# First 512 features of the modulation vector in two halves, with six weight blocks begun between them

## The chip, the cores and the metric

The kernel runs on one core of one Trainium2 chip. A core has a matrix engine (TensorE; PE in the profile, with its weight loads as PEld), a vector engine (VectorE, DVE), a scalar engine (ScalarE, ACT), a general engine (GpSimd, POOL) and a queue engine (SyncE, SP) that here only issues DMAs. Each engine runs its own instructions in the order in which they were written for it, and waits where an instruction needs a result of another engine or a transfer. POOL issues DMAs too, on a queue of its own.

The metric is the time of one execution on the device, in microseconds (us). Three runs of the kernel before took 1944.65, 1945.36 and 1946.12 us; the median is 1945.36 us.

## The reference

One transformer layer on 256 rows of 2048 features, all in float32. A vector c of 2048 numbers gives nine vectors of 2048 numbers each (three shifts, three scales, three gates); they set the modulation of the three parts of the layer:

```python
ada = (jax.nn.silu(c) @ w_ada + b_ada)[:, None, :]
sh1, sc1, g1, sh2, sc2, g2, sh3, sc3, g3 = jnp.split(ada, N_ADA, axis=-1)
h = _swiglu(_modulate(x, sh1, sc1), ffn1_w_in, ffn1_w_out)
x = _layernorm(ALPHA * x + 0.5 * (1 + g1) * h, ln1_g, ln1_b)
h = _token_mixer(_modulate(x, sh2, sc2), w_in, ...)
...
def _modulate(x, shift, scale):
    return _layernorm(x) * (1 + scale) + shift
```

`w_ada` is 2048 x 18432, which is 151 MB, and the feed-forward weights `ffn1_w_in` are 2048 x 11264. So the first matmul of the layer cannot begin before some columns of `w_ada` (shift and scale of the first features) were read over all 2048 rows, summed with silu(c), and put on the normalised x.

## The kernel before, in words

**Precision.** Each float32 operand of a large product is split into two rounded parts, hi (a cast on ACT, L142) and lo (a subtraction on DVE, L143). A product is three matmuls, hi·hi, hi·lo and lo·hi (`mm3`, L357 to L359). x after modulation is kept transposed, as 16 k-tiles of 128 features by 256 rows, each with its hi and lo part (`xhi_f`, `xlo_f`; L296 and L299).

**The opening.** The features of the first feed-forward part are taken in four groups j of 512 (four k-tiles each). For the group j = 0, `first_ada0` reads 16 pieces of `w_ada`, one for each 128 rows of it, with 512 shift and 512 scale columns: 512 KB each, issued by SP (L694). The scale columns are summed on DVE (L155, L157, into `gate`), the shift columns on PE, which multiplies each piece by a column of silu(c) (L695, into `row`). When the last piece is in, the sums over the 128 partitions are made on PE as columns (L658 and L660), DVE adds the bias (`scsh`, L662), ACT applies scale and shift to the transposed x (L293) and casts (L296), DVE makes the lo part (L299). Then the products of group 0 begin. Earlier pieces lie in the buffer `hT`, which later takes partial results, in `gate`, and, for the pieces 12 to 14, in the buffers `araw` and `aw`.

**The products of the opening.** For each group j, twelve blocks i of 512 columns of `ffn1_w_in` are multiplied (`first_in`). A block of a group is 4 k-tiles by 4 column tiles by 3 matmuls: 48 matmuls `s<-...` of 256 columns. Its weights (1 MB) come in one DMA of SP into one of three buffers `raw_s`; hi and lo of two k-tiles each have one of six buffers. The result of a block stands in two of five PSUM banks; for j = 0, ACT copies it to `hT` (L765), for j > 0, DVE adds it there (L767).

**Beside the products.** While group j is multiplied, `first_ada(j + 1)` reads the pieces of the next group (512 KB each, issued by POOL, L721), and DVE sums both of their halves (L155, L157, 1024 elements in each partition). POOL has three buffers for them (two `araw`, one `aw`): a piece is issued when the piece three before has been summed. The columns of the next group (L656 here) are put between the matmuls of the eleventh and twelfth block. Later stages (the rest of the feed-forward part, the mixer, the second feed-forward part) follow on PE without the change touching them.

**Order.** The program is written with generators that are stepped by hand (the tuples of small numbers in the loops say how many pieces are stepped after which block), and a scheduler places the instructions of each engine from that; on each engine the order is then fixed.

Of the kernel before, what the change touches and what calls it, by code (L numbers as in the profile page):

```python
# [14 lines left out]
P = 128  # L15
# [17 lines left out]
def layer_kernel(  # L33
# [304 lines left out]
    def load_w(src, nk, w, name, by_parts=False, behind=None):  # L338
# [4 lines left out]
        h = nk // 2 if nk * w <= 2048 else nk // 4  # L343
# [304 lines left out]
    def first_columns(j, acc, mb, ws, shifts=None):  # L648
        cps = aux_tile(f"cp{j}"), mm_tile(f"cq{j}")

        def column(q):
            cp = cps[q % 2][:, q:q + 2]
            qs = slice(q * P, (q + 1) * P)
# [7 lines left out]
            k = 4 * j + q  # L661
# [4 lines left out]
        column(1)  # L666
        next(mb)
        next(mb)
        column(2)
        next(ws, None)  # L670
        next(mb)
        column(3)
        next(mb)
        for _ in mb:
            pass

    def first_ada0(ws):
        src = pair_cols(0, 0)  # L680
        acc = gate[:, :512]
        part = mm_tile("row0")
        shifts = ap.tile([P, 2, 512], F32, tag="acc", name="shifts")[0:1, 0, :]
        spots = [hT[:, 4 * i:4 * i + 4, :].rearrange("p f t -> p (f t)") for i in range(KF // 4)] + [gate[:, 1024:]]
        spots = [r.rearrange("p (v n) -> p v n", v=2) for r in spots]
        for k in range(KD):
            if k in (12, 13):
                raw = ap.tile([P, 2, 512], F32, tag="araw", bufs=2, name=f"ar0_0_{k}")
            elif k == 14:
                next(ws)  # L690
                raw = ep.tile([P, 2, 512], F32, tag="aw", name=f"ar0_0_{k}")
            else:
                raw = spots[k % 15]
            SP.dma_start(raw, src[k * P:(k + 1) * P])  # L694
            PE.matmul(part[0:1, :], csil[:, k:k + 1], raw[:, 0, :], start=k == 0, stop=k == KD - 1)  # L695
            if k < KD - 1:
                ada_acc(acc, raw[:, 1, :], k)
            else:
                S.copy(shifts, part[0:1, :])
                for b in range(2):  # L700
                    bs = slice(b * 256, (b + 1) * 256)
                    ada_acc(acc[:, bs], raw[:, 1, bs], k)
            if k == 10:
                mb = modulate_both(0, 0, rs0, xT)
            if k in (10, 12):
                next(mb)
            yield
        first_columns(0, acc, mb, ws, shifts)
# [3 lines left out]
    def first_ada(j):  # L712
# [20 lines left out]
        first_columns(j, acc, mb, iter(()))  # L733
# [11 lines left out]
    def first_w(j, i):  # L745
        c0 = (i % 2) * DFF + i // 2 * 512
        for k, hi, lo in load_w(W1[j * 512:(j + 1) * 512, c0:c0 + 512], 4, 512, f"s{j}_{i}",
                                not i + j):
            yield 4 * j + k, hi, lo

    def first_in(j, i, ws):
        gu, q = i % 2, i // 2
        pss = [mm_tile(f"s{j}_{i}_{b}") for b in range(2)]
        ws = list(ws)
        for h in range(2):
            for k, hi, lo in ws:
                for b, ps in enumerate(pss):
                    fs = slice((2 * b + h) * P, (2 * b + h + 1) * P)
                    mm3(ps[:, h * T:(h + 1) * T], hi[:, fs], lo[:, fs], xT[0][:, k, :], xT[1][:, k, :],
                        k == 4 * j, k == 4 * j + 3)  # L760
        for b, ps in enumerate(pss):
            f0 = 2 * NS * gu + 4 * q + 2 * b
            part = first_part(f0, f0 + 2).rearrange("p f t -> p (f t)")
            if j == 0:
# [8 lines left out]

    ws = []


    def ws_halves():
        it = first_w(0, 0)
        for _ in range(2):
            ws.extend(next(it) for _ in range(2))  # L780
            yield

    fa = first_ada0(ws_halves())
# [10 lines left out]
    for k in range(KD):  # L794
        next(fa)
        if k == 4:
# [5 lines left out]
    for j in range(4):  # L802
# [595 lines left out]
```

## Time and profile before

| what | value |
|---|---|
| median of 3 runs | 1945.36 us (1944.65 to 1946.12) |
| profiled execution, its own time | 1941.44 us |
| its span in the profile | 1939.7 us, granted TensorE clock 0.993 of full |
| PE busy | 1897.7 us, 98% of the span |
| DVE busy | 1476.7 us, 76% |
| ACT busy | 944.7 us, 49% |
| read from memory | 506.71 MB |

A line of the part on groups gives the line number, the engine, the operation, the tile written and the tiles read, the shape, how often it came, its busy time, the mean time of one in ns, and the idle time of the engine just before with what ended it. A line of the timeline gives start and duration in us, the engine, the line and the same names; `x3` means three merged instructions, and the bracket is the idle time before and its releaser. A line by windows gives the window, its length, the busy time and count of each engine, then the granted clock, the share of the DMA engines' time, and GB/s. A matmul's own duration is longer than the distance to the next one, since they are pipelined; the distance between starts is what counts.

### The profile page before, as it was taken

Reading aid. Unit: us, or ns where it says so; the run is one execution under the profiler, and the core shown is the slowest. Engines: PE = TensorE matmul, PEld = TensorE weight load, DVE = VectorE, ACT = ScalarE, POOL = GpSimd, SP = SyncE. Lnnn points to the kernel's source line nnn. Section 1 sums busy time; section 2 is a strip of 40 time slices with the busy share of each in tenths; the row PEclk is TensorE's granted clock in tenths of the full one; section 3 lists DMA queues with packets and bytes.
Section 4 is the critical chain, followed back from the end, with each engine's and each line's share of the span. In section 5 each row is a group of like instructions: output and inputs, shape, how many; then the busy total and the mean of one; then the engine's idle time right before and its main releaser. Section 6 shows DMA issues by size and latency. Waiting matters only on the chain.

```text
span 1939.7 us, 32224 instructions
## 1 busy us (share of the span) xinstructions
PE 1897.7 (98%) x13069; PEld 1720.1 (89%) x13069; DVE 1476.7 (76%) x1822; ACT 944.7 (49%) x1330; POOL 54.4 (3%) x82
## 2 busy tenths in 40 slices
PE   6999999999999999999999999999999999999997
PEld 3999999999988888599998785998999999988886
DVE  6789989777788998688988787767766665555776
ACT  3544454444454554745755534655444444444552
POOL 1111100000000000000000000000000000000000
PEclk9999999999999999999999999999999999999998
DMA  9978879999888886499888883987776776655552
GB/s 355 376 272 310 317 232 312 305 311 316 300 316 308 281 296 202 148 315 304 277 295 292 278 306 136 310 292 261 247 254 227 265 239 196 233 186 190 195 195 87
DMA packets 295693, 510.90 MB, mean 263 GB/s; under 512 B 10834, under 2 KB 158706, under 8 KB 294520
## 3 DMA queue, kind: packets, MB, share of 16 engines
q1 hardware_dynamic: 287768, 480.53, 73.3%
q0 software_dynamic: 7776, 28.32, 4.2%
q8 instruction: 102, 1.67, 0.3%
q14 instruction: 47, 0.39, 0.1%
HBM read 506.71 MB, written 2.10 MB: 262 GB/s over the span
## 4 chain that ended last, share of the span: by engine, by line
PE 82%; issue 10%; DMA 4%; DVE 3%; ACT 1%; POOL 0%; SPq 0%; DVEq 0%; ACTq 0%; POOLq 0%
PE gu_f L358 8%; PE gu_f L359 8%; PE o_f L357 8%; PE gu_f L357 8%; PE o_f L359 8%; PE o_f L358 8%; PE s L358 5%; PE s L357 5%; PE s L359 5%; DMA hT<-in_w_ada_dram 2%; PE fh L359 2%; PE fh L357 1%; PE fh L358 1%; PE fs L359 1%; PE fs L358 1%
## 5 line engine op out<-in xcount | busy, mean ns | idle before, releaser
L157 DVE SCALAR_TENSOR_TENSOR acc<-ar,csil,acc 128x1024 f32<-128x1024 f32 x242 | 307.6, 1272 | 86.0 <-DMA ar<-in_w_ada_dram 84.7
L358 PE MATMUL s<-xlo_f,hi_s 128*128 128x256 f32 x768 | 213.2, 278 | 0.3 <-DVE xlo_f L299 0.3
L357 PE MATMUL s<-xhi_f,hi_s 128*128 128x256 f32 x768 | 213.4, 279 | 0.0
L359 PE MATMUL s<-xhi_f,lo_s 128*128 128x256 f32 x768 | 213.0, 277 | 0.0
L359 PE MATMUL gu_f<-xhi_f,lo_f2i 128*128 128x256 f32 x768 | 212.0, 276 | 0.0
L357 PE MATMUL gu_f<-xhi_f,hi_f2i 128*128 128x256 f32 x768 | 212.0, 276 | 0.0
L358 PE MATMUL gu_f<-xlo_f,hi_f2i 128*128 128x256 f32 x768 | 212.0, 276 | 0.0
L143 DVE TENSOR_TENSOR lo_f2i<-raw_f2i,hi_f2i 128x1024 fp32r<-128x1024 f32 x96 | 117.5, 1224 | 89.3 <-ACT hi_f2i L142 89.3
L359 PE MATMUL gu_f<-xhi_f,lo_f1i 128*128 128x256 f32 x640 | 176.7, 276 | 0.0
L357 PE MATMUL gu_f<-xhi_f,hi_f1i 128*128 128x256 f32 x640 | 176.7, 276 | 0.0
L358 PE MATMUL gu_f<-xlo_f,hi_f1i 128*128 128x256 f32 x640 | 176.7, 276 | 0.0
L142 ACT CAST hi_f2i<-raw_f2i 128x1024 fp32r<-128x1024 f32 x96 | 100.8, 1050 | 135.2 <-PE gu_f L358 122.7
L142 ACT CAST hi_s<-raw_s 128x1024 fp32r<-128x1024 f32 x96 | 100.5, 1052 | 130.3 <-PE s L358 92.1
L358 PEld LDWEIGHTS s<-xlo_f,hi_s 128*128 128x128 f32 x768 | 145.1, 189 | 0.6 <-DVE xlo_f L299 0.6
L359 PEld LDWEIGHTS s<-xhi_f,lo_s 128*128 128x128 f32 x768 | 145.0, 189 | 0.0
L357 PEld LDWEIGHTS s<-xhi_f,hi_s 128*128 128x128 f32 x768 | 145.0, 189 | 0.0
L357 PEld LDWEIGHTS gu_f<-xhi_f,hi_f2i 128*128 128x128 f32 x768 | 144.1, 188 | 0.2
L358 PEld LDWEIGHTS gu_f<-xlo_f,hi_f2i 128*128 128x128 f32 x768 | 144.1, 188 | 0.2
L359 PEld LDWEIGHTS gu_f<-xhi_f,lo_f2i 128*128 128x128 f32 x768 | 144.1, 188 | 0.0
L143 DVE TENSOR_TENSOR lo_f2o<-raw_f2o,hi_f2o 128x1024 fp32r<-128x1024 f32 x88 | 107.7, 1224 | 44.9 <-ACT hi_f2o L142 44.8
L142 ACT CAST hh<-hT 128x512 fp32r<-128x512 f32 x130 | 80.0, 622 | 121.4 <-PE o_f L358 120.4
L143 DVE TENSOR_TENSOR lo_s<-raw_s,hi_s 128x1024 fp32r<-128x1024 f32 x96 | 115.6, 1220 | 28.1 <-ACT hi_s L142 28.1
(455 smaller groups left out, 5403.7 us busy)
## 6 DMA issues: line engine op xcount, KB each, us to landing
ar<-in_w_ada_dram SPq DMA_DIRECT2D x227, 512.0 KB, 5.4
raw_f2i<-in_ffn_w_in_dram SPq DMA_DIRECT2D x48, 1024.0 KB, 5.2
raw_s<-in_ffn_w_in_dram SPq DMA_DIRECT2D x47, 1024.0 KB, 7.8
raw_f1o<-in_ffn_w_out_dram SPq DMA_DIRECT2D x44, 1024.0 KB, 7.5
raw_f2o<-in_ffn_w_out_dram SPq DMA_DIRECT2D x44, 1024.0 KB, 5.1
raw_f1i<-in_ffn_w_in_dram SPq DMA_DIRECT2D x40, 1024.0 KB, 7.4
ar<-in_w_ada_dram POOLq DMA_DIRECT2D x48, 512.0 KB, 6.9
raw_mxo<-in_w_out_dram SPq DMA_DIRECT2D x16, 1024.0 KB, 5.7
```

Of the source, the lines that this page charges most:

```text
L142: S.copy(hi, src)
L143: return V.tensor_tensor(out=lo, in0=src, in1=hi.bitcast(F32), op=ALU.subtract)
L157: V.scalar_tensor_tensor(out=acc, in0=raw, scalar=csil[:, k:k + 1], in1=acc, op0=ALU.mult, op1=ALU.add)
L357: PE.matmul(o, ah, bh, start=start, stop=False)
L358: PE.matmul(o, ah, bl, start=False, stop=False)
L359: PE.matmul(o, al, bh, start=False, stop=stop)
```

## The change

The first 512 features come in two halves of 256.

- `first_half` reads 16 pieces of 256 shift and 256 scale columns (256 KB each, L694 of the new file) and sums them as before: scale on DVE, shift on PE. All 16 lie in `hT`. Two columns' worth of modulation (k-tiles 0 and 1) follow from them (`first_columns(0, 0, 2, ...)`).
- `second_half` reads 16 pieces of the other 256 + 256 columns (L715). They lie in parts of `hT` (two of them in `gate`), four of which the first half had used. DVE sums both, 512 elements in each partition; PE takes no part. These give the k-tiles 2 and 3.
- Six blocks of weights (NA = 6) do their products over k-tiles 0 and 1 first, with 512 KB of weights each, and the pieces of the second half are stepped between them. The results of the blocks 0 to 3 (NO = 4) are copied to `hT` by ACT; those of the blocks 4 and 5 stay in PSUM.
- Then the six blocks do k-tiles 2 and 3: first 4 and 5, which go on in their banks and are copied, then 0 to 3, whose result DVE adds to `hT` (L782). Blocks 6 to 11 are done as before, with all four k-tiles.
- The weights' first load comes in two parts of one k-tile each (`h=1`); the others of two k-tiles have one hi and one lo buffer.
- The pieces of group 1 (`first_ada(1)`, POOL) are stepped in `(1, 2, 1, 1, 2, 1)` after the six second visits and `(2, 2, 2, 2, 1, 0)` after blocks 6 to 11; before, it was `(2, 1, 2, 1, 2, 2, 1, 2, 1, 2, 1, 0)` after the twelve blocks. The buffers `araw` and `aw` no longer hold pieces of group 0.

```diff
-    def first_ada0(ws):
-        src = pair_cols(0, 0)
-        acc = gate[:, :512]
...
-        for k in range(KD):
-            if k in (12, 13):
-                raw = ap.tile([P, 2, 512], F32, tag="araw", bufs=2, name=f"ar0_0_{k}")
-            elif k == 14:
-                next(ws)
-                raw = ep.tile([P, 2, 512], F32, tag="aw", name=f"ar0_0_{k}")
-            else:
-                raw = spots[k % 15]
-            SP.dma_start(raw, src[k * P:(k + 1) * P])
...
+    def first_half(ws):
+        src = half_rows(0)
+        acc = gate[:, :256]
...
+        for i, s in enumerate((0, 6, 1, 7, 2, 8, 3, 9)):
+            raw = spots[s]
+            if i == 6:
                 next(ws)
+            for k in range(2):
+                SP.dma_start(raw[:, k], src[2 * i + k])
+                PE.matmul(part[0:1, :256], csil[:, 2 * i + k:2 * i + k + 1], raw[:, k, 0, :], start=i + k == 0,
+                          stop=2 * i + k == KD - 1)
+                if i == 7 and k == 1:
+                    S.copy(shifts, part[0:1, :256])
+                ada_acc(acc, raw[:, k, 1, :], 2 * i + k)
+            if i == 4:
+                first_mb.append(modulate_both(0, 0, rs0, xT))
+            if i in (4, 6):
+                next(first_mb[0])
             yield
+        first_columns(0, 0, 2, acc, first_mb[0], ws, shifts)
+        yield
+
+    def second_half():
+        src = half_rows(1)
+        acc = gate[:, 512:1024].rearrange("p (v n) -> p v n", v=2)
+        for i, s in enumerate((4, 10, 5, 11, 3, 9, 2, 8)):
+            raw = spots[s]
+            for k in range(2):
+                SP.dma_start(raw[:, k], src[2 * i + k])
+                ada_acc(acc, raw[:, k], 2 * i + k)
+            yield
+        first_columns(0, 2, 2, acc, first_mb[0])
         yield
...
+    NA, NO = 6, 4
+    fa = second_half()
+    kept = {}
+    for i in range(NA):
+        with ExitStack() as s:
...
+            kept[i] = first_banks(0, i)
+            first_products(kept[i], first_w(0, i, 0, 2) if i else ws, 0, 1 if i < NO else -1, not i)
+            if i < NO:
+                first_out(0, i, kept[i], False)
+        for _ in range((1, 2, 2, 1, 1, 2)[i]):
+            next(fa, 0)
+    fa = first_ada(1)
+    for n, i in enumerate((*range(NO, NA), *range(NO))):
+        pss = kept[i] if i >= NO else first_banks(0, i)
+        first_products(pss, first_w(0, i, 2, 2), -1 if i >= NO else 2, 3)
+        first_out(0, i, pss, i < NO)
+        more((1, 2, 1, 1, 2, 1)[n])
+    for i in range(NA, NS):
+        first_in(0, i)
+        more((2, 2, 2, 2, 1, 0)[i - NA])
+    for j in range(1, 4):
         fa = first_ada(j + 1) if j < 3 else load_mixer_smalls()
         for i in range(NS):
-            with ExitStack() as s:
-                if j == 0 and i in (1, 2):
-                    s.enter_context(tc.issue_after(x_cast[0]))
-                    s.enter_context(tc.issue_after(pin["x"]))
-                first_in(j, i, ws if i + j == 0 else first_w(j, i))
-            for _ in range((2, 1, 2, 1, 2, 2, 1, 2, 1, 2, 1, 0)[i] if j < 3 else i not in (4, 9, 11)):
-                with pinned():
-                    next(fa, 0)
+            first_in(j, i)
+            more((2, 1, 2, 1, 2, 2, 1, 2, 1, 2, 1, 0)[i] if j < 3 else i not in (4, 9, 11))
```

More of the change, by code (lines that the diff above doesn't have):

```diff
@@ L335, in new_xT, with load_w @@
         return (xp.tile([P, KD, T], F32R, name=f"xhi_{tag}"), xp.tile([P, KD, T], F32R, name=f"xlo_{tag}"))
-    def load_w(src, nk, w, name, by_parts=False, behind=None):
+    def load_w(src, nk, w, name, by_parts=False, behind=None, h=None):
         raw = wp.tile([P, nk, w], F32, tag="raw", bufs=3, name=f"raw_{name}")
@@ L644, in layer_kernel, with first_columns, column @@
     W1 = ffn1_w_in[0]
[L648 to L653, printed above, removed]
+    def first_columns(j, q0, nq, acc, mb, ws=(), shifts=None):
+        cps = aux_tile(f"cp{j}_{q0}"), mm_tile(f"cq{j}_{q0}")
+        ws = iter(ws)
+        def column(i):
+            cp = cps[i % 2][:, i:i + 2]
+            qs = slice(i * P, (i + 1) * P)
             for v in range(2):
@@ new lines, in first_columns, with half_rows @@
+        for i in range(1, nq):
+            column(i)
+            next(mb)
+            next(ws, None)
+            next(mb)
+        next(mb, None)
+    def half_rows(g):
+        src = w_ada[0, :, 0:2 * D].rearrange("(k p) (v n) -> k p v n", p=P, v=2)
+        return src[:, :, :, g * 256:(g + 1) * 256]
+    spots = [hT[:, 4 * i:4 * i + 4, :].rearrange("p f t -> p (f t)") for i in range(KF // 4)] + [gate[:, 1024:]]
+    spots = [r.rearrange("p (k v n) -> p k v n", k=2, v=2) for r in spots]
+    first_mb = []
@@ L732, in first_ada @@
             yield
-        first_columns(j, acc, mb, iter(()))
+        first_columns(j, 0, 4, acc, mb)
         yield
@@ L763, in first_in @@
             part = first_part(f0, f0 + 2).rearrange("p f t -> p (f t)")
-            if j == 0:
+            if not add:
                 S.copy(part, ps)
@@ L772, in first_in, with ws_parts @@
                     V.tensor_tensor(out=hT[:, f - 2 * NS, :], in0=sg, in1=first_part(f, f + 1)[:, 0, :], op=ALU.mult)
+    def first_in(j, i):
+        pss = first_banks(j, i)
+        first_products(pss, first_w(j, i), 4 * j, 4 * j + 3)
+        first_out(j, i, pss, j > 0)
     ws = []
[L777 to L780, printed above, removed]
+    def ws_parts():
+        for w in first_w(0, 0, 0, 2):
+            ws.append(w)
             yield
-    fa = first_ada0(ws_halves())
+    fa = first_half(ws_parts())
     rs0 = [small(3, "mr", f"mr_x{a}") for a in range(2)]
@@ L793, in layer_kernel @@
                                op0=ALU.mult, op1=ALU.mult)
-    for k in range(KD):
+    for i in range(8):
         next(fa)
-        if k == 4:
+        if i == 2:
             load_bcol()
```

68 lines of the change are left out of this document (26 added, 42 removed).

## The prediction

> **What bounds the kernel now.** I read the page first, then busy time by windows, then PE's waits, then the timeline of the opening.
>
> ```profile
> span 1939.7 us, 32224 instructions
> PE 1897.7 (98%) x13069; PEld 1720.1 (89%) x13069; DVE 1476.7 (76%) x1822; ACT 944.7 (49%) x1330; POOL 54.4 (3%) x82
> ```
> ```profile
> 0.00:36.00 36.00, 21.32 (x56) 5.20 (x56) 19.82 (x40) 5.91 (x9) 5.14 (x14) 0.99 0.97 359
> 36.00:42.00 6.00, 5.70 (x26) 5.39 (x26) 3.91 (x9) 5.11 (x9) 0.26 (x1) 0.50 1.04 384
> 42.00:107.00 65.00, 65.00 (x573) 65.00 (x573) 50.08 (x50) 39.98 (x58) 11.30 (x16) 1.00 0.97 344
> 107.00:175.00 68.00, 68.00 (x602) 68.00 (x601) 61.72 (x71) 30.64 (x37) 12.14 (x17) 1.00 0.88 310
> ```
> ```profile
> PE s L358 <- DVE xlo_f L299: 0.3, 1, 0.3
> ```
>
> PE sets the time: 65.00 of 65.00 us busy, a matmul each 0.113 us (68.00 / 602), and in 36 to 320 us its only wait is 0.3 us. So an earlier start of the matmuls is a gain if no stall follows. But in group 0 (42 to 107 us) the cover is thin: DVE works 50.08 of 65 us, the DMA engines 97%.
>
> ```profile
> 21.26 1.02 PE L695 MATMUL row<-hT,csil 128*1 128x512 f32 x2 [0.34 <-DMA hT<-in_w_ada_dram]
> 28.04 1.02 PE L695 MATMUL row<-ar,csil 128*1 128x512 f32 x2 [0.34 <-DMA ar<-in_w_ada_dram]
> 28.11 0.89 POOL L721 DMA_DIRECT2D ar<-in_w_ada_dram  x1 [13.88 <-DMA ar<-in_w_ada_dram]
> 30.75 1.02 PE L695 MATMUL row<-ar,csil 128*1 128x512 f32 x2 [1.69 <-DMA ar<-in_w_ada_dram]
> 31.58 0.75 DVE L157 SCALAR_TENSOR_TENSOR gate<-ar,csil,gate 128x512 f32<-128x512 f32 x1
> 32.11 1.02 PE L695 MATMUL row<-hT,csil 128*1 128x512 f32 x2 [0.34 <-DMA hT<-in_w_ada_dram]
> 33.16 0.57 ACT L699 COPY shifts<-row 1x512 f32<-1x512 f32 x1 [2.75 <-PE row L695]
> 34.52 0.16 DVE L662 TENSOR_TENSOR scsh<-cp,bcol 128x2 f32<-128x2 f32 x1 [1.27 <-PE cp L658]
> 34.77 0.56 ACT L293 ACTIVATE xf<-tp,scsh 128x256 f32<-128x256 f32 x1 [1.04 <-DVE scsh L662]
> 35.37 0.40 ACT L296 CAST xhi_f<-xf 128x256 fp32r<-128x256 f32 x1
> 36.92 0.56 PE L357 MATMUL s<-xhi_f,hi_s 128*128 128x256 f32 x1
> 39.27 0.58 PE L358 MATMUL s<-xlo_f,hi_s 128*128 128x256 f32 x1 [0.30 <-DVE xlo_f L299]
> 42.47 0.28 PE L357 MATMUL s<-xhi_f,hi_s 128*128 128x256 f32 x1
> ```
>
> Pieces land every (28.04 - 21.26) / 5 = 1.356 us, the last at 32.1; the first product starts at 36.92. The granted clock is 0.50 until 42; matmuls come each 0.21 us there. By 42.47 24 were done (the first two windows and the rows between), as if PE had begun at full clock at 42.47 - 24 x 0.113 = 39.75. One later mark is needed: the columns of group 1, before the twelfth block.
>
> ```profile
> 100.79 0.34 PE cp L656 x4
> ```
>
> **The change part by part.**
>
> *First half lands.* Sixteen pieces of 256 KB replace sixteen of 512 KB. The runs shrink from 2 to 1 KB. Bounds: 0.68 us (half of 1.356) and a dearer small packet:
>
> ```profile
> DMA packets 6445, 14.47 MB, mean 362 GB/s; under 512 B 412, under 2 KB 572, under 8 KB 6189
> q1 hardware_dynamic: 6013, 12.90, 87.1%
> ...
> DMA packets 43110, 55.62 MB, mean 309 GB/s; under 512 B 1155, under 2 KB 35971, under 8 KB 43095
> q1 hardware_dynamic: 42999, 55.07, 92.3%
> ```
>
> These are the windows 0 to 40 and 320 to 500 us: 0.871 x 16 x 40 / 6013 = 92.7 ns for 2145 B, 0.923 x 16 x 180 / 42999 = 61.8 ns for 1281 B; the line through both gives 52.6 ns for 1 KB against 89.2 for 2 KB, 0.59 of a piece, 0.80 us. I take 0.75, since these means hold crowded stretches. The Trainium skill ("DMA: Bandwidth & Descriptors", Specifications) asks only for 512 B for full rate; by it a piece costs 0.68 us and the half would land 1.1 us sooner. The two windows speak against full equality.
>
> Also moved: POOL's pieces of group 1. Before, the first waits until 28.11 for `araw`. After, `araw` and `aw` are free and in the new instruction order the first stands ahead of all POOL's waits, two more behind the first row statistic: three transfers of 512 KB, 3 x 1.356 = 4.07 us, now share the engines before the half is in. Ahead of the last piece stands 256 instead of 512 KB of weights. Landing: 32.1 - 16 x (1.356 - 0.75) - 0.68 + 4.07 = 25.8 us. SP issues 32 instead of 16 pieces at under 0.7 us each, hidden by the landings.
>
> *First product.* PE's last row product is halved (0.5), the copy 0.4, then as before from copy to `scsh`, `xf`, `xhi`: 28.9 us. At the low clock 24 matmuls take 5.1 us: block 0 ends at 34.2 (31.6 at full clock; what follows hangs on DVE and changes by under 1 us).
>
> *Between the halves.* DVE is the queue to follow, in its new order. Prices: lo 1.22 us (1.14 between starts), a group-1 piece 1.28 (1.20), a copy 0.59, an add 0.68 (0.60), a second-half piece 0.75:
>
> ```profile
> L143 DVE TENSOR_TENSOR lo_s<-raw_s,hi_s 128x1024 fp32r<-128x1024 f32 x95 | 114.4, 1219 | 26.5 <-ACT hi_s L142 26.5
> L767 DVE TENSOR_TENSOR hT<-hT,s 128x512 f32<-128x512 f32 x66 | 42.1, 679 | 0.0
> L765 ACT COPY hT<-s 128x512 f32<-128x512 f32 x22 | 11.8, 586 | 0.3
> ...
> 42.49 1.28 DVE L157 SCALAR_TENSOR_TENSOR acc<-ar,csil,acc 128x1024 f32<-128x1024 f32 x1
> 36.58 1.04 ACT L142 CAST hi_s<-raw_s 128x1024 fp32r<-128x1024 f32 x1
> ```
>
> The second half's shift columns move from PE to DVE, 16 x 0.75 = 12 us of DVE among the lo parts. Walk: hi of block 2 waits on ACT behind block 0's copies (36.4), its lo ends at 37.6; four second-half pieces stand ahead of lo of block 3, which ends at 41.8, so PE, at block 3 since 40.0, waits 1.3; blocks 4 and 5 end at 46.8 and 49.9 (0.4 waited). The last second-half piece landed at 45.1 and was summed by 48.3, so it isn't late. But its columns stand in PE's order behind block 5: 0.5 us to `scsh`, two `xf` in a row, `xhi`; k-tile 2 starts at 52.2 and PE idles 1.9 us. So 144 matmuls are done at 52.2, as if begun at 52.2 - 16.3 = 35.9: the gain stands at 39.75 - 35.9 = 3.9 us.
>
> *Second visits and block 6.* Six visits of 24 keep PE busy until 52.2 + 16.3 = 68.5. In DVE's order, eight group-1 pieces and eight new adds (L782, 8 x 0.60 = 4.8 us that ACT's copies did not cost DVE) stand ahead of block 6's second lo. From 53.0: 0.75 + 4 x 1.14 + 7 x 1.20 + 8 x 0.60 + 2 x 1.14 = 20.8 us, and 1.1 of waits for ACT's casts: 74.9. PE has 12 matmuls of block 6, then 12 and 8 transposes taken forward from later blocks, until 72 to 73, and the forward ones count; so block 6 waits about 2.9 us net: gain 3.9 - 2.9 = 1.0.
>
> *Blocks 6 to 11.* From 74.9 DVE alternates piece and lo. POOL keeps three pieces under way, and before one took 6.9 us to land:
>
> ```profile
> ar<-in_w_ada_dram POOLq DMA_DIRECT2D x16, 512.0 KB, 6.9
> ```
>
> (6.9 + 0.8 of issue) / 3 = 2.57 us a pair against 1.20 + 1.14 = 2.34: the lo of block 8 comes 0.6 us late, those of 9 and 10 in time. Net 0.4 us: the columns of group 1 stand at about 100.4 instead of 100.79. From there each queue's order is the old one, and PE has no waits to give back. On the profiled execution 1941.44 - 0.4 = 1941.0; the median of the runs is 3.9 us above it, so 1945.
>
> **The rivals.** *DVE keeps pace (faster).* If DVE's waits on ACT and on order are smaller than I walked, block 6 has its lo parts by 70 us and only the 1.9 us at the columns stay: from 52.2, gain 3.9; with the waits between the halves gone as well (k-tile 2 at 49.9), 6.2. For it: DVE has 15 us free in 42 to 107. Against it: 12 us of second-half sums and 4.8 of adds go into that room, and the stretch begins earlier. Time 1939 to 1941.5. It decides when block 6's second lo is done before 72.
>
> *Pieces of group 1 come late (slower).* The eighth stands ahead of block 6's second lo. It is issued when the fifth was summed (67.7). At 6.9 us and 0.7 for issue it lands at 75.3, the lo ends at 77.7: 2.8 more. The next pairs run at 2.57 or worse at 97% DMA, 1 to 2 more. PE idles 4.7 us at a stretch there; in the row of 36 to 42 us the granted clock was 0.50 after a thin stretch, and 6 us at half clock cost 3. Sum 2.8 + 2 + 3 - 0.4 = +7.4, or +4.4 without the clock: 1950 to 1953. The Trainium skill ("TensorE: Matmul & The Clock Gate", Part 1) lets the clock fall to half after about 3.4 us of idling; by that rule this rival pays the 3 us, and my forecast's 2.9 us stall doesn't. For it: the 6.9 us row. Against: between 66 and 75 us no weights may load (their buffers wait for the same lo), so POOL's pieces should land faster. It decides at about 4.5 us from issue to landing.
>
> *The half doesn't land earlier.* If the three POOL transfers took more than their share, nothing changes in the bytes: 25.8 holds them whole. So this stays within the range.
>
> **How the numbers follow.** 0.2% is 3.9 us, about what a measurement of this kernel can tell from no change. No change, within 1941.5 to 1949.2: 0.43. DVE keeps pace, faster by more than that: 0.25. Late pieces, slower by more: 0.32; I give it more than the fast one since my walk took most transfers as punctual. The likeliest is 1945 with a range of its own of 1941.5 to 1949.2; the range for 8 in 10 goes down to 1939 (most of the fast rival) and up to 1951.5 (more than half of the slow one).
>
> **What would show it.** Last piece of the first half at 25 to 27 us, first `s` matmul near 29; PE idle of 1 to 2 us at block 3 and at the columns L657; `s` of block 6 waiting for DVE's lo around 72 to 75; columns of group 1 near 100; adds of L782 and `gate` sums filling DVE over 90% from 28 to 95. Wrong if PE shows no wait on DVE after 55 us (fast rival), or if DVE itself waits for `ar` there and the clock shows 0.50 (slow rival).

## The result, and the profile after

The changed kernel takes 1954.14 us (median of five runs, 1950.07 to 1958.73), the kernel before 1944.65 us (five runs, 1943.41 to 1946.12). The ratio is 1.0048 with a 95% interval of 1.0034 to 1.0061: slower by some 9.5 us, where no change was forecast, and above the upper end of the range (1951.5). The profiled execution of the changed kernel took 1950.07 us, 8.6 more than that of before; its trace can explain those 8.6.

The page's head, and busy time by windows over the same stretches as in the prediction (length; busy us of PE, PEld, DVE, ACT, POOL with their instructions; granted clock; DMA share; GB/s):

```profile
span 1948.4 us, 32309 instructions
PE 1896.8 (97%) x13069; PEld 1723.3 (88%) x13069; DVE 1487.4 (76%) x1846; ACT 945.8 (49%) x1331; POOL 54.3 (3%) x82
```
```profile
0.00:36.00 36.00, 21.00 (x94) 11.18 (x95) 21.61 (x49) 9.51 (x15) 4.89 (x14) 0.95 0.99 337
36.00:42.00 6.00, 4.57 (x36) 3.97 (x34) 5.33 (x7) 3.09 (x5) 0.00 (x0) 1.00 1.07 367
42.00:107.00 65.00, 57.55 (x475) 56.23 (x475) 53.01 (x56) 31.80 (x42) 11.61 (x16) 0.97 0.93 325
107.00:175.00 68.00, 65.50 (x562) 65.31 (x562) 57.40 (x65) 31.85 (x39) 10.14 (x14) 0.97 0.82 291
...
42.00:60.00 18.00, 16.63 (x140) 16.37 (x141) 15.75 (x20) 13.09 (x19) 2.19 (x3) 1.00 0.85 276
```

In 42 to 107 us PE works 57.55 instead of 65.00 us and gets 475 instead of 573 matmuls done. The DMA engines, 97% busy there before, move 325 instead of 344 GB/s: 19 x 65 = 1.2 MB less. What is missing is missing in 42 to 60 us, where the share is 0.85 and 276 GB/s are moved (1.01 and 356 before, so 80 x 18 = 1.4 MB less), most of all in 48 to 54 us. The rows of that stretch, first before, then after, and what POOL did at its end:

```profile
48.00:54.00 6.00, 6.00 (x55) 6.00 (x55) 5.22 (x5) 3.46 (x6) 1.44 (x2) 1.00 0.96 365
```
```profile
48.00:54.00 6.00, 4.84 (x40) 4.71 (x40) 4.59 (x9) 4.95 (x8) 0.00 (x0) 1.00 0.64 187
...
54.34 0.75 POOL L731 DMA_DIRECT2D ar<-in_w_ada_dram  x1 [40.24 <-DVE acc L155]
```

POOL has idled 40.24 us when it issues here: its three buffers hold pieces of group 1 that DVE sums only behind the second half. Before, it issued five pieces from 41.74 to 52.82 us.

The timeline of the changed kernel, around the first half's end and at three marks (the first product, the 145th, which is the first of k-tile 2, and the 577th, the first of group 1):

```profile
24.64 0.59 PE L695 MATMUL row<-hT,csil 128*1 128x256 f32 x2 [0.16 <-DMA hT<-in_w_ada_dram]
25.39 0.59 PE L695 MATMUL row<-hT,csil 128*1 128x256 f32 x2 [0.16 <-DMA hT<-in_w_ada_dram]
...
26.18 0.48 DVE L157 SCALAR_TENSOR_TENSOR gate<-hT,csil,gate 128x256 f32<-128x256 f32 x1 [0.26 <-DMA hT<-in_w_ada_dram]
...
29.21 0.50 PE L357 MATMUL s<-xhi_f,hi_s 128*128 128x256 f32 x2 [0.73 <-ACT xhi_f L296]
...
52.52 0.39 PE L357 MATMUL s<-xhi_f,hi_s 128*128 128x256 f32 x1 [1.16 <-ACT xhi_f L296]
...
118.03 0.28 PE L357 MATMUL s<-xhi_f,hi_s 128*128 128x256 f32 x1
```

In the kernel before the same three stand at 36.92, 56.10 and 107.93 us. So the products of the first two k-tiles are 3.6 us ahead at the second mark (56.10 - 52.52), and 10.1 us behind at the third: 13.7 us are lost in between. Of the 10.1 us, 8.6 are left at the end. PE's waits of 28 to 125 us (total, times, longest):

```profile
PE s L357 <- DVE hT L782: 2.9, 2, 1.9
PE cp L657 <- DVE scsh L663: 2.5, 1, 2.5
PE s L359 <- DVE lo_s L143: 2.5, 3, 1.3
PE s L357 <- ACT xhi_f L296: 1.9, 2, 1.2
PE s L357 <- ACT hT L780: 1.7, 1, 1.7
PE s L357 <- ACT hi_s L142: 0.5, 1, 0.5
```

Where they lie, and what stands ahead of the instruction that PE waits for, in the timelines of ACT, DVE and PE:

```profile
65.82 1.99 ACT L142 CAST hi_s<-raw_s 128x1024 fp32r<-128x1024 f32 x2 [4.24 <-DMA raw_s<-in_ffn_w_in_dram]
66.90 1.23 DVE L143 TENSOR_TENSOR lo_s<-raw_s,hi_s 128x1024 fp32r<-128x1024 f32 x1 [1.67 <-ACT hi_s L142]
68.04 1.28 DVE L782 TENSOR_TENSOR hT<-hT,s 128x512 f32<-128x512 f32 x2
68.77 0.38 PE L357 MATMUL s<-xhi_f,hi_s 128*128 128x256 f32 x1 [1.90 <-DVE hT L782]
...
75.33 1.28 DVE L157 SCALAR_TENSOR_TENSOR acc<-ar,csil,acc 128x1024 f32<-128x1024 f32 x1
75.44 0.36 PE L357 MATMUL s<-xhi_f,hi_s 128*128 128x256 f32 x1 [1.05 <-DVE hT L782]
76.53 1.22 DVE L143 TENSOR_TENSOR lo_s<-raw_s,hi_s 128x1024 fp32r<-128x1024 f32 x1
77.80 0.50 PE L359 MATMUL s<-xhi_f,lo_s 128*128 128x256 f32 x2 [1.33 <-DVE lo_s L143]
...
99.52 1.04 ACT L142 CAST hi_s<-raw_s 128x1024 fp32r<-128x1024 f32 x1 [5.05 <-DMA raw_s<-in_ffn_w_in_dram]
100.47 1.07 ACT L780 COPY hT<-s 128x512 f32<-128x512 f32 x2
101.10 0.39 PE L357 MATMUL s<-xhi_f,hi_s 128*128 128x256 f32 x1 [1.71 <-ACT hT L780]
...
108.41 1.04 ACT L142 CAST hi_s<-raw_s 128x1024 fp32r<-128x1024 f32 x1 [1.10 <-DMA raw_s<-in_ffn_w_in_dram]
109.49 1.23 DVE L143 TENSOR_TENSOR lo_s<-raw_s,hi_s 128x1024 fp32r<-128x1024 f32 x1 [0.92 <-ACT hi_s L142]
110.63 0.15 DVE L663 TENSOR_TENSOR scsh<-cp,bcol 128x2 f32<-128x2 f32 x1
110.84 0.61 PE L657 MATMUL cp<-trir,acc 128*128 128x1 f32 x4 [2.50 <-DVE scsh L663]
```

Read each group from its end. At 68.77 PE, three matmuls into block 3's second visit, gets its second bank when the add of block 1 frees it; that add stands on DVE behind the lo of block 6, which waits for ACT's cast, which waits for the weights of block 6. At 77.80 PE waits for block 6's second lo, which stands behind sums of group 1's pieces and adds. At 101.10 a copy that frees a bank stands on ACT behind a cast that waited 5.05 us for weights. At 110.84 the columns of group 1 wait for a 0.15 us addition which DVE could have done at once, had it not stood behind a lo of group 1's second block, whose weights had only just landed. Three of the four are work that PE needed now, behind a cast for a block that PE came to some 3 us (block 6, at 71.3) to 13 us later.

The two groups of waits also cost clock. Windows of the changed kernel, columns as above:

```profile
74.00:78.30 4.30, 1.92 (x15) 1.46 (x14) 4.27 (x5) 1.20 (x2) 1.45 (x2) 1.00 0.75 219
78.31:81.72 3.41, 3.41 (x18) 3.41 (x18) 3.41 (x4) 0.00 (x0) 0.87 (x2) 0.50 0.83 262
...
108.00:112.40 4.40, 1.90 (x17) 1.71 (x16) 2.45 (x7) 3.99 (x7) 0.00 (x0) 1.00 0.90 314
112.44:115.86 3.42, 3.42 (x19) 3.42 (x18) 2.33 (x5) 1.98 (x6) 0.00 (x0) 0.50 0.54 165
```

In 3.41 us at full clock 30 matmuls would run (0.113 us each), and 18 and 19 did: 23 x 0.113 = 2.6 us. With the five waits after 53 us (1.90 + 1.05 + 1.33 + 1.71 + 2.50 = 8.5) that is 11.1 of the 13.7. Each of the five restarts also costs 0.16 us more than its wait, between the last start and the idle time; the rest is in gaps under 0.3 us and slower steps around the restarts.

### The profile page after: what moved, and what is told of

The parts are those of the page before. It is cut to its first block, busy times and chain, and to the rows that moved or that the text cites. A ratio compares the mean times of both kernels' runs of the same rounds, so it can differ in the third digit from the quotient of the medians.

```text
span 1948.4 us, 32309 instructions
## 1 busy us (share of the span) xinstructions
PE 1896.8 (97%) x13069; PEld 1723.3 (88%) x13069; DVE 1487.4 (76%) x1846; ACT 945.8 (49%) x1331; POOL 54.3 (3%) x82
## 3 DMA queue, kind: packets, MB, share of 16 engines
q8 instruction: 102, 1.67, 0.3%
## 4 chain that ended last, share of the span: by engine, by line
PE 78%; issue 11%; DMA 5%; DVE 4%; ACT 1%; POOL 0%; SPq 0%; DVEq 0%; ACTq 0%; POOLq 0%
PE gu_f L357 8%; PE gu_f L359 8%; PE o_f L357 8%; PE gu_f L358 8%; PE o_f L359 8%; PE o_f L358 8%; PE s L359 4%; PE s L357 4%; PE s L358 3%; DMA ar<-in_w_ada_dram 2%; DMA hT<-in_w_ada_dram 2%; PE fh L358 1%; PE fh L357 1%; PE fh L359 1%; PE fs L357 1%
## 5 line engine op out<-in xcount | busy, mean ns | idle before, releaser
L142 ACT CAST hi_s<-raw_s 128x1024 fp32r<-128x1024 f32 (+1 forms) x97 | 100.5, 1042 | 128.6 <-PE s L358 86.2
L357 PE MATMUL o_f<-hi_f2o,hh 128*128 128x512 f32 x344 | 135.2, 393 | 0.0
```

What stands on the lines that cost most here:

```text
L142: S.copy(hi, src)
L357: PE.matmul(o, ah, bh, start=start, stop=False)
```

## The experiments

Each ratio is against runs of the kernel before made together with the experiment (medians 1942.9 to 1945.4 us), with its 95% interval. All edits are made on the changed kernel, which is at 1.0048 (1.0034 to 1.0061) itself; two edits whose intervals overlap are not told apart by them.

**First set: one suspected cause at a time.** Theory A: weights late because half loads (0.5 MB) leave the three 1 MB buffers half filled. Theory B: DVE's order, with eight pieces of group 1 and eight adds ahead of block 6's second lo. Theory C: the transfers of group 1's pieces.

*Two half loads share a buffer.*

```diff
+        if nk == 2 and not start:
+            if not shared:
+                both = wp.tile([P, 4, 512], F32, tag="raw", bufs=3, name=f"raw_s{j}_{i}_{k0}")
+                shared.extend((both[:, 0:2], both[:, 2:4]))
+            raw = shared.pop(0)
```

> Two half loads of 0.5 MB share one buffer of 1 MB, so SP can have six of them under way instead of three; nothing else is changed. Theory A (the weights come late from 58 us on, because three buffers half filled let the DMA engines idle: busy share 0.85 and 276 GB/s in 42 to 60 us): that share goes to 0.95 or more, ACT's longest waits for raw_s between 60 and 110 us (4.24 and 5.05 us) shrink below 2.5, the columns of group 1 come at 103 to 107 instead of 110.8, and the time is 3 to 7 us under the changed kernel's 1954.1: 1947 to 1951. Theory B (DVE's order: eight pieces of group 1 and eight adds ahead of block 6's second lo): no change, 1951 to 1956, and block 6's second lo still ends at 76 to 78. Theory C (the pieces of group 1 themselves land late): no gain or a loss, as more weights under way slow them: 1953 to 1958.

Measured 1953.67 us, 1.0039 (1.0024 to 1.0055): a miss for A; B's time came in, and its mark too (block 6's second lo ends at 77.24). The DMA share in 42 to 60 us rose only to 0.89 and the wait of 68.77 us was gone, but PE waited 4.0 us for a cast at block 6, 2.9 for a bank at block 10, and 2.7 at the columns.

*Fewer pieces early.*

```diff
-        more((1, 2, 1, 1, 2, 1)[n])
+        more((1, 0, 1, 0, 1, 0)[n])
...
-        more((2, 2, 2, 2, 1, 0)[i - NA])
+        more((3, 3, 3, 3, 2, 0)[i - NA])
```

> Three instead of eight pieces of group 1 are stepped during the second visits, the others after blocks 6 to 11; the bytes are the same. Theory B: block 6's second lo ends at 70 to 72 instead of 77.75, PE's stalls between 66 and 78 us (2.2, 0.4, 1.3, 1.6) and the stretch at clock 0.50 behind them go, 4 to 6 us: 1948 to 1950. Theory A: the weights are as late as before, and more pieces stand in 80 to 107 us, so the columns of group 1 come no earlier than 110.8: 1952 to 1960. Theory C: the same as A, at its upper end.

Measured 1955.36 us, 1.0050 (1.0035 to 1.0066). Between 53 and 98 us PE did not wait at all, so B's place was real; then the columns waited 8.6 us in one piece for the last pieces of group 1. The loss had moved, and A's range came in instead of B's.

*Sums of group 1's pieces left out.*

```diff
+            if j == 1 and k:
+                ada_acc(acc[:, :, 0:16], raw[:, :, 0:16], k)
```

> Every transfer stays; of the pieces of group 1 after the first, DVE sums only 16 of 512 columns (the rest of group 1's shift and scale sums is left out), which takes some 15 x 1.0 us from DVE. Theory B: with DVE free, the stalls between 66 and 78 us and the one of 2.8 at the columns go: 1943 to 1947. Theory A: ACT still waits for raw_s (4.2 at 66, 5.0 at 99 us) and PE behind it; only what lay on DVE alone is won, 1 to 4 us: 1950 to 1953. Theory C: as A.

*Loads of group 1's pieces left out.*

```diff
+            if j == 1 and k > 2:
+                raw = kept_raws[k % 3]
+            else:
+                raw = where.tile([P, 2, 512], F32, tag=tag, bufs=n, name=f"ar0_{j}_{k}")
+                G_.dma_start(raw, src[k * P:(k + 1) * P])
+                kept_raws[k % 3] = raw
```

> DVE's sums and their order stay, but the pieces of group 1 after the third aren't loaded (sums take the first three again, so those of thirteen k-tiles are left out): 13 x 0.5 MB or some 19 us of all DMA engines less. Theories A and C: no transfer is late any more, ACT's waits for raw_s go under 1 us, and the time is 1941 to 1946. Theory B: block 6's second lo stands behind as many sums and ends at 74 to 76; the stalls at 66 to 78 us stay, those at 99 and 108 may go: 1947 to 1951.

Without the sums: 1952.04 us, 1.0049 (1.0034 to 1.0063). Without the loads: 1950.70 us, 1.0032 (1.0016 to 1.0047). The first is in the range of A and C, the second in that of B. Neither the smaller sums nor 6.5 MB less on the DMA engines brings all of the time back; in the traces the first product of group 1 stands at 115.92 and 111.77 instead of 118.03 us. The windows 60 to 107 us say why, first without the sums, then without the loads:

```profile
60.00:107.00 47.00, 41.09 (x360) 40.70 (x359) 26.59 (x39) 21.96 (x29) 9.39 (x13) 0.97 1.02 378
```
```profile
60.00:107.00 47.00, 42.55 (x359) 41.53 (x359) 40.22 (x43) 23.94 (x32) 2.19 (x3) 0.98 0.71 252
```

Without the sums DVE works 26.59 of 47 us, and the DMA engines are full (1.02, 378 GB/s). Without the loads the DMA share is 0.71, and DVE works 40.22 of 47 us. ACT still waits 10.6 us for weights in 60 to 112 us there (22.4 in the changed kernel, 8.7 before), although the DMA engines have room: SP's longest wait for a `lo` part that frees a weight buffer is 12.2 us. Each limit is there behind the other.

**Second set: both limits.** Theory D: two limits of like size, DVE's queue and the DMA engines. Theory E: the bytes on the DMA engines alone. Theory F: only the order, with columns behind casts of later blocks.

*All the sums left out (second half and group 1), or those of the second half alone.*

```diff
+                if i + k:
+                    ada_acc(acc[:, :, 0:16], raw[:, k, :, 0:16], 2 * i + k)
```

> Left out: DVE's sums of 496 of the 512 columns of every piece of the second half and of group 1 but the first (some 9 us between 28 and 49 us and 15 us after 53); every transfer stays. Theory D (two limits of like size, DVE's queue and the DMA engines: DVE's late lo parts hold the raw buffers, so the DMA engines idle in 42 to 60 us, busy share 0.85, and can't make it up later): the share in 42 to 60 rises to 0.95 or more, and since DVE is free all along only the DMA limit is left: 1944 to 1949. Theory E (the DMA engines alone, short by 0.9 MB at 42 us for the 1-KB runs): as without the sums of group 1 alone, 1950 to 1953. Theory F (only the order: the columns of group 1 stand behind lo parts of later blocks): 1950 to 1953, with a wait over 4 us at the columns.

> Left out: the sums of 496 of 512 columns of the second half's pieces alone (some 9 us of DVE between 28 and 49 us). Theory D: the waits at blocks 2 and 3 go, k-tile 2 starts by 50.5 instead of 52.5, the DMA share in 42 to 60 us is 0.95 or more, and 3 to 6 us come back: 1948 to 1951. Theory E: the 2 us at k-tile 2 only are won and lost again at the columns: 1952 to 1955. Theory F: as E.

Measured 1951.32 us, 1.0034 (1.0018 to 1.0050), and 1958.20 us, 1.0079 (1.0048 to 1.0110). D missed both; for the first, E's and F's numbers came in, with a wait of 4.6 us at the columns. The DMA share in 42 to 60 us did not rise (0.79 and 0.81), so smaller sums between the halves did not fill the engines there. Both edits also changed the order: in both traces PE waits 1.8 us for a cast at block 1, which had moved behind block 0's copies on ACT, and k-tile 2 starts at 54.4 and 53.9 us. So these two runs do not single out the sums. That the second would be slower than the changed kernel was expected by none; the intervals overlap, and whether the cast is the whole of it stays open.

*Neither loads nor sums of group 1's pieces.* The edits of the two runs of the first set together.

> Left out: the loads of group 1's pieces after the third (6.5 MB) and the sums of 496 of 512 columns of its pieces after the first. Theory D: both limits gone after 53 us, the first product of group 1 starts at 102 to 106 us instead of 118, and the time is 1938 to 1943, below the kernel before. Theory E: as without the loads alone, 1947 to 1951. Theory F: the order is kept, so the columns still wait 2 to 5 us: 1946 to 1950.

Measured 1939.78 us, 0.9974 (0.9957 to 0.9991): faster than the kernel before. Its windows, and two marks of its timeline (first product of k-tile 2, first of group 1):

```profile
52.36:55.77 3.41, 3.41 (x16) 3.41 (x17) 3.03 (x7) 3.41 (x5) 0.00 (x0) 0.50 0.76 242
55.77:107.00 51.23, 51.23 (x453) 51.23 (x453) 32.75 (x49) 31.04 (x45) 2.19 (x3) 1.00 0.78 268
```
```profile
52.31 0.56 PE L357 MATMUL s<-xhi_f,hi_s 128*128 128x256 f32 x1 [1.15 <-ACT xhi_f L296]
...
105.78 0.28 PE L357 MATMUL s<-xhi_f,hi_s 128*128 128x256 f32 x1
```

PE has no wait from 53 to 125 us, and group 1 begins at 105.78 instead of 107.93. (This trace is of an execution of 1945.22 us; it is ahead of the kernel before at every mark up to the last product of the first matmul, at 307.86 against 309.99 us, and loses 5.9 us behind it, where the two do the same work.) So the early start is a gain of its own, as the prediction's fast rival had it, if group 1's pieces cost nothing. D's number came in, and F's rule (the columns wait in any case) fell.

*Second visits copied by ACT instead of added by DVE.*

```diff
-        first_out(0, i, pss, i < NO)
+        first_out(0, i, pss, False)
```

> The second visits of blocks 0 to 3 are copied out by ACT, as before the change, instead of added by DVE (the first visits' part is lost): eight adds of 0.6 us less on DVE, eight copies more on ACT. Theory D: block 6's second lo no longer stands behind adds that wait for PE; it ends 4 to 6 us earlier, at 71 to 73, but the DMA limit takes most of it: 1950 to 1953. Theory E: no change, 1952 to 1956. Theory F: no change.

Measured 1950.24 us, 1.0023 (1.0003 to 1.0042): by the medians half of the loss, with every transfer and sum of the pieces in place. In 60 to 75 us the DMA share was 1.03 instead of 0.95, and block 6's second lo ends at 72.88. D's forecast came in; E and F, which expected no change, missed.

**Third set: the order.** Theory G: weights that are a little late become PE's waits because work needed at once stands behind casts for later blocks.

*At the columns: lo parts of group 1's first two blocks, and hi of its second, behind the columns.*

```diff
+                if after_cols == 2:
+                    s.enter_context(tc.issue_after(x_cast[0]))
+                S.copy(hi, part)
+                if after_cols:
+                    s.enter_context(tc.issue_after(cols[1]))
```

> Only the order is changed: the lo parts of group 1's first two blocks, and the hi parts of its second, go behind the columns of group 1 in DVE's and ACT's queues; nothing is left out. Theory G (the lateness of weights becomes PE's because work needed at once stands behind casts of blocks needed 5 to 10 us later): the 2.77 us wait at the columns and the 3.41 us at clock 0.50 behind it go, and 3 to 5 us come back: 1949 to 1951. Theory E (bytes alone): PE meets the missing weights at group 1's first blocks instead, 1952 to 1956.

*That, and block 6's weights cast ahead of the adds of blocks 2 and 3.*

```diff
+        w = ahead.pop(i, None) or first_w(0, i, 2, 2)
+        first_products(pss, w, -1 if i >= NO else 2, 3)
+        if i == NO - 2:
+            ahead[i + 1] = list(first_w(0, i + 1, 2, 2))
+            ahead[NA] = list(first_w(0, NA))
```

> The order at the columns as in the run before, and block 6's weights (and block 3's second half) are cast ahead of the adds of blocks 2 and 3 and of the group 1 pieces behind them. Nothing is left out. Theory G: block 6's second lo ends by 72 instead of 77.75, SP's next load starts by as much earlier, and 5 to 8 us come back in all: 1946 to 1949. Theory E: raw for block 9 starts earlier, but the DMA engines were 0.95 to 0.97 busy already, so 1951 to 1955.

*Four two-visit blocks instead of six, with the order at the columns.*

```diff
-    NA, NO = 6, 4
+    NA, NO = 4, 2
...
-        for _ in range((1, 2, 2, 1, 1, 2)[i]):
+        for _ in range((2, 2, 2, 3)[i]):
...
-        more((1, 2, 1, 1, 2, 1)[n])
+        more((1, 2, 1, 2)[n])
...
-        more((2, 2, 2, 2, 1, 0)[i - NA])
+        more((1, 2, 1, 2, 2, 2, 1, 0)[i - NA])
```

> Four blocks instead of six do their first two k-tiles ahead of the second half, two instead of four of them are added up (four adds instead of eight), with the order at the columns as above. Nothing is left out. The second half lands some 2.5 us earlier (1 MB of weights less ahead of it), PE idles 5 to 7 us before k-tile 2 at about 48.5 us, so the gain there is 2 instead of 3.9 us, and DVE has 2.4 us less to do. Theory G: no stall at block 4 over 1 us; 1944 to 1949. Theory E: DMA as short as before, 1950 to 1955.

*Copies instead of adds, with the order at the columns.* The edits of two runs above together.

> Both orders mended at once, with work left out: second visits copied by ACT instead of added by DVE (the first visits' part is lost), and the order at the columns as above. Theory G: the two places are the whole loss, 1943 to 1947. Theory E: 1948 to 1951, as without the adds alone.

Measured in turn: 1953.01 us, 1.0037 (1.0017 to 1.0057); 1949.03 us, 1.0019 (1.0003 to 1.0036); 1951.63 us, 1.0030 (1.0014 to 1.0046); 1945.93 us, 1.0014 (0.9993 to 1.0034). The columns alone bring nothing that the interval can tell (a miss for G's number, while E's came in): in that trace the wait at the columns is gone, but the waits for banks at 70 and 77 us are 2.8 and 1.0, and one of 2.3 stands at 103. With both orders half of the loss is back, by the medians. Without the adds and with the order, nothing is left that can be measured, and PE has one wait after 53 us, 3.8 for a bank at block 3's second visit, and works 32.00 of 32 us in 75 to 107. With four two-visit blocks k-tile 2 starts at 49.0 us, near the 48.5 expected, but PE still waits 1.4 us for a cast at 62 us and 2.0 for a bank at 92; E's range came in.

**Fourth set: order and read-ahead together.** Nothing is left out in these.

*Both orders, and shared buffers.*

> The mended order at the columns and at block 6, and two half loads to a buffer. Nothing is left out. Theory G with late weights from half-filled buffers: block 6's weights may be asked for when block 0's instead of block 1's second half is cast (some 2.3 us earlier), PE's wait at 68 us goes under 1, and 1 to 3 us come back from 1949.0: 1945 to 1948. Theory E: no change, 1948 to 1951.

*The same with seven instead of eight pieces in the second visits.*

```diff
-        more((1, 2, 1, 1, 2, 1)[n])
+        more((1, 1, 1, 1, 1, 2)[n])
...
-        more((2, 2, 2, 2, 1, 0)[i - NA])
+        more((3, 2, 2, 2, 1, 0)[i - NA])
```

> As the run before, with one instead of two pieces of group 1 stepped after the second visits of blocks 5 and 2, and so five instead of seven pieces ahead of block 7's lo. Nothing is left out. If the pieces' transfers make block 6's weights late: another 1 to 3 us, 1943 to 1947. If not: later pieces make PE wait at the columns instead, 1946 to 1950.

*Both orders, shared buffers, four two-visit blocks.*

> As the run of both orders and shared buffers, with four two-visit blocks instead of six. Nothing is left out. If DVE's work (four adds less, 2.4 us) is what is left: 1942 to 1946. If not: the 5 us that PE idles before the second half cost 1 to 2 us, 1947 to 1951.

Measured 1947.12 us, 1.0019 (1.0001 to 1.0037); 1944.91 us, 1.0008 (0.9988 to 1.0028); 1946.12 us, 1.0015 (1.0001 to 1.0029). In the trace of the first PE still waits 2.6 us for a `lo` part at 79 us and 2.7 for a bank at 84.5, and group 1 begins at 114.04. The second can't be told from the kernel before; group 1 begins at 110.54 there. Its PE waits of 53 to 125 us, which were five of 8.5 us in the changed kernel:

```profile
PE cp L667 <- DVE acc L157: 1.8, 1, 1.8
PE s L365 <- ACT hT L799: 0.3, 1, 0.3
```

**Fifth set: buffers for the pieces.** The one wait left is for the last pieces of group 1. Two or four pieces go into parts of `hT` that are free from the second half on.

```diff
+            if j == 1 and k in {3: 3, 4: 9}:
+                raw = spots[{3: 3, 4: 9}[k]].rearrange("p k v n -> p (k v n)").rearrange("p (v n) -> p v n", v=2)
```

> As the last run but one (both orders, shared buffers, seven pieces in the second visits), and two of group 1's pieces are loaded into parts of hT that the second half has left and that blocks 6 and 7 write only after 76 us. Nothing is left out. If the late pieces are what is left: DVE's waits for ar after 60 us (4.0 in all) go under 1.5, the stall at the columns goes, and the time is 1940 to 1943, below the kernel before by 0.1 to 0.2%. If the DMA engines as a whole are: 1944 to 1947.

> The same with four pieces, two of them issued from 35 us on, while the second half lands. Late pieces: 1939 to 1943. If the two early transfers hold up the second half (2 x 1.36 us), k-tile 2 starts 1 to 2.5 us later, 1943 to 1946.

> Four pieces in hT, and the changed kernel's own placing of the steps (eight in the second visits). Late pieces: as the run before, 1939 to 1943. If pieces summed early hold up lo parts on DVE: 1944 to 1948.

Measured 1945.23 us, 1.0014 (0.9999 to 1.0028); 1948.64 us, 1.0025 (1.0014 to 1.0035); 1946.86 us, 1.0020 (1.0008 to 1.0033). None is faster than the kernel before. With four early pieces, two of them on their way while weights and second half land, k-tile 2 comes 5.2 us after the 52.52 of the changed kernel; rows of the second run of this set:

```profile
43.64 0.47 PE L365 MATMUL s<-xhi_f,hi_s 128*128 128x256 f32 x1 [3.31 <-ACT hi_s L357]
...
57.72 0.39 PE L365 MATMUL s<-xhi_f,hi_s 128*128 128x256 f32 x1 [1.15 <-ACT xhi_f L296]
```

The wait at 57.72 is the changed kernel's own (1.16 there). What is new is the 3.31 at block 3, whose cast waited 4.80 us for its weights, and 6.83 us at clock 0.50 behind it. The DMA share in 42 to 60 us is 0.99: the idle room is used, and PE waits earlier for it. So the room was filled at the cost of weights needed earlier, which is the part of theory E that is left; whether a better order of the transfers would gain is not shown. No version was found that is faster than both kernels with all its work done.

## Why the prediction was wrong

Point by point, by its own steps:

- *Piece of the first half, 0.75 us; landing 25.8.* Right: PE's row products follow at 24.64 and 25.39, 0.75 apart, and DVE's last sum waits for its piece until 26.18. The rule of the Trainium skill that it was weighed against ("DMA: Bandwidth & Descriptors", Specifications: full rate from 512 bytes, 0.68 us) does not hold in these rows.
- *First product 28.9, k-tile 2 at 52.2, gain 3.9.* Right: 29.21, 52.52, 3.6. The waits between the halves were of the forecast size too.
- *Second visits until 68.5 without a wait.* Wrong: the wait of 1.90 at 68.77. The walk gave 1.1 us to all waits for ACT's casts ahead of block 6's second lo; two alone took 1.77 and 1.67 us on DVE (61.61 and 66.90). The second was for block 6, whose weights landed at 65.8 (ACT's row), and the add that frees a bank stood behind it.
- *Block 6's second lo at 74.9, PE waits 2.9.* The place was right, the size was not: it ran from 76.53 to 77.75, and PE waited 1.90 + 1.05 + 1.33 on the way, with 1.4 us for the clock behind these short waits, which the forecast did not price. The forecast's gain falls from 3.9 to 0.4 by block 9 (2.9, and 0.6 for block 8). Measured, the first product of block 9 stands at 93.45 against 89.63 us before: from 3.6 ahead to 3.8 behind.
- *Blocks 6 to 11: block 8's lo 0.6 late, "those of 9 and 10 in time"; columns of group 1 at 100.4.* This is the step that failed, and the one before it with it: the walk followed pieces and `lo` parts, and put the weights of blocks 9 to 11 at nothing. The prediction had said itself that no weights may load between 66 and 75 us, since their buffers wait for the same lo, and gave it no price. In the trace SP waited for that lo:

```profile
SPq L342 <- DVE lo_s L143: 16.1, 3, 11.9
```

This is of 60 to 80 us; the load behind the 11.9 is that of block 9, issued at 77.77. ACT then waited 3.14, 2.26 and 5.05 us for the weights of blocks 9, 10 and 11. Its first cast for a block stood 5.4 to 7.7 us ahead of the block's first product for blocks 6, 9, 10 and 11; before, this was 7.9 to 11.5 us for blocks 6 to 11. With that little in hand the order of the queues counts: a copy stood behind block 11's cast, and the columns behind the lo of group 1's second block, 1.71 + 2.50 us and 1.2 of clock. The columns came at 110.84. "From there each queue's order is the old one, and PE has no waits to give back" held: PE is 10.1 us behind at group 1's first product and 10.6 at the last one of this matmul.

- *Why the weights were late.* "My walk took most transfers as punctual" is the assumption under both wrong steps. In 48 to 54 us the DMA share is 0.64 where before had 0.96: the second half is in, SP's loads wait for `lo` parts, and POOL can't issue until DVE reaches the first piece of group 1 (the 40.24 us). Extra buffers for pieces, which let POOL issue earlier (from 30.75 us on with four), raised the share in 42 to 60 us from 0.90 to 0.94 with two and 0.99 with four, and from 0.80 to 0.99 with the changed kernel's steps; sharing the weight buffers gave 0.89 alone instead of 0.85; smaller sums on DVE did not raise it. So buffers that come free late account for the idle room; that it is the whole reason why block 6's weights came late is not shown.

The slow rival came nearest (1950 to 1953 against 1954.14), with the half clock, block 6's lo (77.7 forecast, 77.75 measured) and the landing of the eighth piece (75.3 and 75.23). Much of that is luck: by its mechanism PE waits for late pieces, but the pieces took 6.7 us at the median (6.9 before), DVE had work up to the eighth and took it up without a wait, and with the transfers after the third left out the ratio is still 1.0032. DVE did wait for pieces later, 4.3 us in all from 83 us on, as the rival's sign had it; PE's waits there hang on weights.

What is shown: either the pieces' sums or their transfers are enough for a loss (1.0032 without the transfers, 1.0049 without the sums), and with both away it turns into a gain. With no work less, the time can't be told from the kernel before once four things are mended together: the order at block 6, the order at the columns, the half-filled buffers, and one piece less in the second visits (1.0008); without the last it is 1.0019 (1.0001 to 1.0037). What each of the four is worth is not shown, as their intervals overlap. Nor does the early start become a gain there: in the trace of that run group 1 begins at 110.54, 2.6 us later than before.

The changed kernel's runs lie 1950 to 1959 apart, and only the one of 1950.07 has a trace here. Much of such a spread can come from later stages: from the last product of the first matmul to the end, where the kernels do the same work, the traces of this case take 1626 to 1639 us (1629.8 before, 1627.7 changed).

## What to carry to other kernels

In this kernel the order of the in-order queues cost nothing as long as casts stood some 8 us and more ahead of their products; when the change ate into that, casts for later blocks that stand ahead of a copy, an add or a small sum became the matrix engine's waits. So when work is started earlier, ask not only whether each engine has room but how many us of weights stay ahead, and look in each queue for what PE needs now behind what it needs later. Where two resources are both near full, removing the load of one can leave most of the time where it is: take both away before a cause is ruled out, and mend both places before a repair is.

## What was unexpected of the hardware

The granted clock fell to 0.50 for 3.41 us after waits much shorter than that: no wait between 74.00 and 78.30 us was over 1.33 us (PE busy 1.92 of 4.30), and the clock was 0.50 right after; in the run without loads and sums it was so behind a single wait of 1.15 us ahead of 52.31. But the like wait of 1.16 us ahead of 52.52 in the changed kernel was not followed by it, nor was the 1.71 ahead of 101.10; in the run of both orders PE was busy 2.33 of 4.00 us in 66 to 70 us, and no half clock followed. Within a trace the stretches at 0.50 lie on a grid: those of the changed kernel ahead of 125 us start at 30.52, 78.31 and 112.44 us, which is 14 and 10 times 3.413 us apart. In the piece of that grid just ahead of such a stretch PE was busy 1.53 us (74.90 to 78.31) and 1.60 us (109.03 to 112.44), and 2.26 us in the run without loads and sums (48.96 to 52.37); 98.79 to 102.20, with 1.70 us, was not followed by one. So the length of a wait alone does not decide; these rows suggest that its place on the grid counts too, and how much idling is needed is not shown. The prediction had taken from the Trainium skill ("TensorE: Matmul & The Clock Gate", Part 1) that it takes about 3.4 us of idling; the length of the slow stretch agrees with the page's window, the idling needed does not agree in these rows.

Smaller runs cost bandwidth here even with the engines full. A packet of 1 KB took 51 ns on average in 14 to 26 us of the changed kernel, one of 2 KB 89 ns in the same stretch before: 1.74 times as long for twice the bytes. In 0 to 42 us the DMA share was 0.98 before and 1.01 after, and 363 against 341 GB/s were moved, with 1 KB instead of 2 KB at a time for the first features:

```profile
0.00:42.00 42.00, 27.03 (x80) 10.59 (x81) 23.73 (x48) 11.02 (x17) 5.39 (x15) 0.92 0.98 363
```
```profile
0.00:42.00 42.00, 25.57 (x127) 15.15 (x127) 26.94 (x55) 12.60 (x20) 4.89 (x14) 0.96 1.01 341
```

The first row is of the kernel before, the second of the changed one: 22 x 42 = 0.9 MB, 2.7 us of transfers at 341 GB/s.
